# FFN input products by one Strassen step on a normalised input, with the preceding output products in token halves

## The chip, the cores and the metric

The kernel runs on one core of a Trainium2 chip. What counts is the device time of one execution in microseconds (us), as the median of several runs. The engines that matter are TensorE (PE, matrix products into PSUM), VectorE (DVE), ScalarE (ACT), GpSimd (POOL) and the DMA queues, of which SyncE's (SP) carries the weights.

## The reference

The kernel computes one inference step of a two-layer backbone for 640 tokens (512 latent, 128 context) of width 1024. Each layer is FFN 1, a mixer (pooling, convolution, attention) and FFN 2. Cut to the part that the change touches:

```python
m = silu(cond) @ mod_w + mod_b                # 9 modulation vectors of 1024, per layer and kind of token
def ffn(x, shift, scale, gate, wi, wo):       # wi 1024 x 5632, wo 2816 x 1024
    h = rms(x, norm_g) * (1 + scale) + shift  # rms: x / sqrt(mean(x*x)) * norm_g
    g, up = split(h @ wi, 2)                  # two times 2816 columns
    return x + 0.5 * gate * ((silu(g) * up) @ wo)
# per layer: x = ffn 1; x = x + g2 * concat(pool, conv, attn) @ w_out; x = ffn 2
```

All data are float32.

## The kernel before

X holds the residual stream transposed: 8 chunks of 128 features by 640 tokens. Every product in float32 is made as three products of two parts: a matrix is rounded to a high part (`f_wh`, `f_h`, a ScalarE copy) and the rest becomes a low part (`f_wl`, a VectorE subtraction), and high by high, high by low and low by high are summed in PSUM. The 640 tokens are two halves of 320, one PSUM bank each.

An FFN has 44 input chunks of 128 columns (22 of the gate, 22 of the other factor, named `f{layer}{place}_{pair}_{part}{chunk}`; a pair is 256 columns of each part). A weight tile `wi` of 1 MB holds 256 columns; `raw` tiles have three buffers. A chunk is 8 × 3 × 2 = 48 matmuls (line 356). The moving operand `xa` is X times the modulation's scale, not normalised, and two further columns hold the shift; the factor 1/rms (`R`, lines 300 to 313) is multiplied into the product's output in PSUM (lines 392 and 393), the shift's share is added there too, and silu, the gating (line 436) and the split of the hidden chunk (lines 438 and 439) follow. The output products run in four groups of hidden chunks (`GROUPS`, 6, 6, 6 and 4), each over the 8 output chunks m, and each adds into X (line 398, `o_a` and `o_b` are the two halves). A group of output products stands one pair of input chunks behind the hidden chunks that it reads.

The modulation vectors are 72 loads of 1 MB (`mw`). Those at the start are products of 64 columns (line 259). Most of the others are "summed": eight VectorE rows per load accumulate into `ma` (line 225), then a few small products. The code calls one such step at each input weight tile and each pair of output chunks while steps are left (`more`), others inside the mixer.

A scheduler with a look-ahead of 200 (`AHEAD`) arranges each engine's instructions; the order in this document is what it made. The rows of the end of the mixer and of the end of an FFN update X chunk by chunk and at once prepare the next `xa` chunk (`xa_chunk`) and the sum of squares (`sq_chunk`, GpSimd line 382).

Of the kernel before, what the change touches and what calls it, by code (L numbers as in the profile page):

```python
# [95 lines left out]
def backbone(ctx: ExitStack, tc: tile.TileContext, ins, consts, y_prompt, y_sample, out_k, out_v):  # L96
# [106 lines left out]
    def modulation(l, v, summed):  # L203
# [3 lines left out]

        def step(t):
            raw = wpool.tile([P, 2, D], F32, tag="raw", name=f"mw_{l}_{v}_{t}", bufs=3)
# [4 lines left out]
            if summed:  # L214
                if t == 0:
                    st["acc"] = [[half(f"ma_{l}_{v}_{i}{q}") for q in range(2)] for i in range(2)]
                for kk in range(2):
                    k = 2 * t + kk
                    for i in range(2):
                        for q in range(2):  # L220
                            acc, src, c = st["acc"][i][q], raw[:, kk, 512 * q:512 * q + 512], C[:, k, i:i + 1]
                            if k == 0:
                                V.tensor_scalar(out=acc, in0=src, scalar1=c, scalar2=None, op0=ALU.mult)
                            else:
                                V.scalar_tensor_tensor(out=acc, in0=src, scalar=c, in1=acc, op0=ALU.mult, op1=ALU.add)
                if t < 3:
                    return
                ps = bank(f"mod_{l}_{v}", "x")
                for q in range(2):
                    for i in range(2):  # L230
                        w = st["acc"][i][q].rearrange("p (j g c) -> p j g c", g=4, c=32)
                        for g in range(4):
                            PE.matmul(ps[32 * g:32 * g + 32, 128 * q:128 * q + 128], pick[i], w[:, :, g, :], start=(i == 0), stop=(i == 1))
            else:
                if t == 0:
                    st["ps"] = bank(f"mod_{l}_{v}", "x")
                ps = st["ps"]
                for kk in range(2):
                    k = 2 * t + kk
                    w = raw[:, kk, :].rearrange("p (j g c) -> p j g c", g=4, c=32)  # L240
                    for g in range(4):
                        PE.matmul(ps[32 * g:32 * g + 32, 0:256], C[:, k, :], w[:, :, g, :], start=(k == 0), stop=(k == KD - 1))
                if t < 3:
                    return
            mt = half(f"modT_{l}_{v}", 256)
            V.transpose(out=mt, in_=ps[:, 0:256])
            b = mod_b[l][:, v * KD:(v + 1) * KD].unsqueeze(2).to_broadcast([P, KD, 2])
            V.tensor_tensor(out=modv[l][:, v], in0=mt.rearrange("p (j c) -> p j c", c=32)[:, :, 0:2], in1=b, op=ALU.add)
# [743 lines left out]
```

## Time and profile before

| what | value |
|---|---|
| timed runs, median of 3 | 2519.34 us (2518.88 to 2521.01) |
| profiled execution | 2518.95 us |
| its span, first to last instruction | 2517.2 us |
| mean granted TensorE clock | 0.984 of full speed |
| TensorE busy | 2438.6 us, 97% |
| VectorE busy | 1441.7 us, 57% |
| ScalarE busy | 823.5 us, 33% |
| GpSimd busy | 214.1 us, 9% |

The span is shorter than the time, since it counts from the first to the last instruction alone. Busy shares are means over stages with different limits.

### The profile page before, as it was taken

What the parts mean: (1) busy time and instruction counts of PE and PEld (TensorE: products, weight loads), DVE (VectorE), ACT (ScalarE), POOL (GpSimd) and SP (SyncE); (2) the same over time, 40 slices, a digit from 0 to 9 for tenths busy, and PEclk for the clock granted to TensorE, in tenths of its full rate; (3) what the DMA queues carried; (4) which work ended last, traced back from release to release, by engine and by line L of the source; (5) the groups of instructions that cost most, each with busy time, mean ns of one, the idle gap of its engine ahead of it and who ended that gap; (6) DMA issues with size and microseconds to landing.
All of it is one profiled execution on the core that took longest, in us unless ns stands there. A gap on an engine that the chain in (4) does not pass through costs nothing. (4 is left out here: it accounts for less than half of the span.)

```text
span 2517.2 us, 40160 instructions
## 1 busy us (share of the span) xinstructions
PE 2438.6 (97%) x17151; PEld 2343.7 (93%) x17151; DVE 1441.7 (57%) x2878; ACT 823.5 (33%) x1334; POOL 214.1 (9%) x168
## 2 busy tenths in 40 slices
PE   7999999999879999999999999999997899999999
PEld 6999999998569999999999999999885799999999
DVE  6774434468858877734374443446598664444444
ACT  3222222236664222212242122224357542121212
POOL 2000000012531000000010000001124210000000
PEclk8999999999889999999999999999999899999999
DMA  9443222233503344422132222222333131212222
GB/s 291 143 147 107 64 82 67 68 103 107 178 26 114 138 133 152 151 84 68 59 95 74 76 76 76 76 68 76 117 107 130 43 101 59 93 59 84 68 67 68
DMA packets 195919, 245.10 MB, mean 97 GB/s; under 512 B 5721, under 2 KB 178558, under 8 KB 195740
## 3 DMA queue, kind: packets, MB, share of 16 engines
q1 hardware_dynamic: 193904, 240.81, 29.1%
q8 instruction: 134, 2.20, 0.4%
q0 software_dynamic: 368, 1.07, 0.1%
q10 hardware_dynamic: 1468, 0.66, 0.1%
q14 instruction: 45, 0.37, 0.0%
HBM read 239.63 MB, written 2.88 MB: 96 GB/s over the span
## 5 line engine op out<-in xcount | busy, mean ns | idle before, releaser
L356 PE MATMUL f_a<-xa_h,f_wl 128*128 128x320 f32 x1384 | 430.5, 311 | 2.9 <-DVE f_wl L336 2.9
L356 PE MATMUL f_a<-xa_h,f_wh 128*128 128x320 f32 x1384 | 431.2, 312 | 1.1 <-DVE f_t L392 0.7
L356 PE MATMUL f_b<-xa_h,f_wh 128*128 128x322 f32 x1384 | 432.0, 312 | 0.0
L356 PE MATMUL f_b<-xa_h,f_wl 128*128 128x322 f32 x1384 | 431.5, 312 | 0.0
L356 PE MATMUL f_b<-xa_l,f_wh 128*128 128x322 f32 x1384 | 430.6, 311 | 0.2 <-DVE xa_l L374 0.2
L356 PE MATMUL f_a<-xa_l,f_wh 128*128 128x320 f32 x1384 | 429.2, 310 | 0.0
L356 PE MATMUL o_a<-f_h,o_wh 128*128 128x320 f32 x1408 | 423.4, 308 | 0.0
L356 PE MATMUL o_b<-f_h,o_wh 128*128 128x320 f32 x1408 | 422.9, 308 | 0.0
L335 ACT ACTIVATE f_wh<-wi 128x1024 fp32r<-128x1024 f32 x175 | 185.4, 1060 | 705.0 <-PE f_b L356 460.9
L392 DVE TENSOR_TENSOR f_t<-f_a,r 128x320 f32<-128x320 f32 x176 | 86.0, 491 | 540.2 <-PE f_a L356 537.9
L356 PEld LDWEIGHTS f_a<-xa_h,f_wl 128*128 128x128 f32 x1384 | 262.1, 189 | 4.9 <-DVE f_wl L336 3.9
L356 PEld LDWEIGHTS f_a<-xa_h,f_wh 128*128 128x128 f32 x1384 | 262.8, 190 | 2.9 <-ACT f_wh L335 1.1
L356 PEld LDWEIGHTS o_a<-f_h,o_wh 128*128 128x128 f32 x1408 | 263.6, 187 | 1.2 <-ACT o_wh L335 1.0
L356 PEld LDWEIGHTS o_b<-f_h,o_wh 128*128 128x128 f32 x1408 | 263.6, 187 | 0.0
L356 PEld LDWEIGHTS f_a<-xa_l,f_wh 128*128 128x128 f32 x1384 | 262.1, 189 | 0.0
L356 PEld LDWEIGHTS f_b<-xa_h,f_wh 128*128 128x128 f32 x1384 | 261.8, 189 | 0.4 <-issue 0.3
L356 PEld LDWEIGHTS f_b<-xa_l,f_wh 128*128 128x128 f32 x1384 | 261.1, 189 | 0.5 <-DVE xa_l L374 0.5
L356 PEld LDWEIGHTS f_b<-xa_h,f_wl 128*128 128x128 f32 x1384 | 261.0, 189 | 0.2
L335 ACT ACTIVATE o_wh<-wo 128x768 fp32r<-128x768 f32 (+1 forms) x128 | 101.2, 792 | 438.7 <-PE o_b L356 309.0
L336 DVE TENSOR_TENSOR f_wl<-wi,f_wh 128x1024 fp32r<-128x1024 f32 x175 | 215.2, 1230 | 12.2 <-ACT f_wh L335 8.2
L398 DVE SCALAR_TENSOR_TENSOR X<-o_a,gate,X 128x320 f32<-128x320 f32 x128 | 70.2, 549 | 259.9 <-PE o_a L356 259.7
L356 PE MATMUL o_a<-f_h,o_wl 128*128 128x320 f32 x704 | 217.0, 308 | 1.9 <-DVE o_wl L336 1.7
(420 smaller groups left out, 3976.2 us busy)
## 6 DMA issues: line engine op xcount, KB each, us to landing
wi<-in_ffn_wi_dram SPq DMA_DIRECT2D x86, 1024.0 KB, 5.2
mw<-in_mod_w_dram SPq DMA_DIRECT2D x72, 1024.0 KB, 5.8
wo<-in_ffn_wo_dram SPq DMA_DIRECT2D x48, 768.0 KB, 4.7
wo<-in_ffn_wo_dram SPq DMA_DIRECT2D x16, 512.0 KB, 3.6
wout<-in_w_out_dram SPq DMA_DIRECT2D x32, 256.0 KB, 3.0
win_q<-in_w_in_dram SPq DMA_DIRECT2D x4, 1024.0 KB, 5.0
xt<-in_x_sample_dram SPq DMA_DIRECT2D x4, 512.0 KB, 5.8
wi<-in_ffn_wi_dram SPq DMA_DIRECT2D x4, 512.0 KB, 10.1
```

The source lines that it names most:

```text
L335: A.activation(out=wh, in_=src, func=AF.Copy)
L336: V.tensor_tensor(out=wl, in0=src, in1=wh.bitcast(F32), op=ALU.subtract)
L356: PE.matmul(ps[:, :n], ww[:, k, :], xx[:, lo:lo + n], start=(k == order[0] and i == 0), stop=(k == order[-1] and i == 2))
L392: V.tensor_tensor(out=t[:, :HALF], in0=pa[:, :HALF], in1=R[:, :HALF], op=ALU.mult)
L398: V.scalar_tensor_tensor(out=X[:, m, s:e], in0=ps[:, s - o:e - o], scalar=gate[:, m, c:c + 1], in1=X[:, m, s:e], op0=ALU.mult, op1=ALU.add)
```

## The change

The input products of an FFN are made by one step of Strassen's scheme in Winograd's form. The contraction is taken in pairs of 128-feature blocks (even and odd, four pairs kp), a group of 256 columns in two halves, and the tokens in two halves; of eight products of blocks, seven are left, called P1, P2, q6, n5, q7, m4 and q3 (`FORMS`). For this:

- The input is normalised, scaled and shifted before the products (`rstd_half`, `half_input`), since the scheme adds blocks of both token halves. From it seven combinations per k-pair are made and split (`forms_first` for the first half, `forms_second` when the second is there).
- For each group g of 22 per FFN the weights are seven half tiles of 512 columns per partition (`weights`: a ScalarE copy and a VectorE subtraction); four are sums of blocks, t1 and t2 on VectorE, t3 and t4 on GpSimd (`sums`, `run`).
- The products' results are combined on VectorE (in `run`, `second`, `last`): V, U, then the four blocks. The product m4 of a group stands in the next group (`late`).
- The output products that feed an FFN's input (the mixer's last part, and FFN 2's last group in layer 0) run first for tokens 0 to 319, then for 320 to 639 (`last_group`); the first half is normalised meanwhile, and P1 and P2 of the first two groups (`early`) stand before the second half's normalisation (`into_ffn`).
- The modulation steps stand at places that are listed (`fill`): after groups 1 to 5 of the first FFN, and after the odd m of the first two or three output groups of three FFNs; a summed step now takes 512 columns of four k-blocks. At the start all eight modulation tiles come before any product.
- `raw` has two buffers instead of three, split weights three instead of two, `act` six instead of eight. Tiles of an FFN and of a mixer share one region (`phase`), and a table of constants is loaded per mixer.

```diff
-BUFS = {"act": 8, "tmp": 7, "half": 9}
+BUFS = {"act": 6, "tmp": 7, "half": 9, "w": 3, "raw": 2}
...
+        def weights(self, g, form, src):
...
+            h, lo = self.slots.pop(0)
+            A.activation(out=h, in_=src, func=AF.Copy)
+            V.tensor_tensor(out=lo, in0=src, in1=h.bitcast(F32), op=ALU.subtract)
...
+            V.tensor_tensor(out=t1, in0=self.block(g, 0, 0), in1=self.block(g, 0, 1), op=ALU.add)
+            V.tensor_tensor(out=t2, in0=t1, in1=self.block(g, 1, 1), op=ALU.add)
+            G.tensor_tensor(out=t3, in0=self.block(g, 1, 1), in1=self.block(g, 0, 1), op=ALU.add)
...
+            for kp in range(4):
+                for n, (w, f) in enumerate(((h, 0), (h, 1), (lo, 0))):
+                    PE.matmul(ps[:, :HALF], w[:, kp, :], self.F[f][kp][:, i, :], start=(first and kp == 0 and n == 0), stop=(kp == 3 and n == 2), skip_group_check=not first)
...
+            t1, t2, t3 = self.sums(g)
+            self.weights(g, "q6", t2)
+            self.multiply(g, "q6", d, True)
+            V.tensor_tensor(out=v, in0=d[:, :HALF], in1=v, op=ALU.subtract)
+            G.tensor_tensor(out=t2, in0=t2, in1=self.block(g, 1, 0), op=ALU.add)
+            st["t4"] = t2
+            self.weights(g, "n5", t1)
+            self.multiply(g, "n5", B, True)
+            u = half(nm + "_U", HALF)
+            V.tensor_tensor(out=u, in0=B[:, :HALF], in1=v, op=ALU.add)
+            if self.late is not None:
+                self.last(self.late)
+            self.weights(g, "q7", t3)
+            self.multiply(g, "q7", Cb, True)
+            V.tensor_tensor(out=o[1][:, HALF:], in0=Cb[:, :HALF], in1=u, op=ALU.add)
+            if not done:
+                self.second(g)
+            self.weights(g, "q3", self.block(g, 1, 1))
+            self.multiply(g, "q3", B, False)
+            V.tensor_tensor(out=o[1][:, :HALF], in0=B[:, :HALF], in1=v, op=ALU.add)
+            self.hidden(g, 1, slice(0, T))
...
+        def then(h):
+            if h == 1:
+                for g in range(2):
+                    f.early(g)
+            pb = rstd_half(acc, h, f"r{l}{j}{h}")
+            for kp in range(4):
+                if h == 0:
+                    hp.append(forms_first(F, af, pb, kp, f"hf{l}{j}"))
+                else:
+                    forms_second(F, af, pb, kp, hp[kp], f"hf{l}{j}")
...
+        V.tensor_tensor(out=g[:, 0], in0=hq[:, 0], in1=hq[:, 1], op=ALU.add)
+        V.tensor_tensor(out=g[:, 1], in0=hp[:, 0], in1=g[:, 0], op=ALU.subtract)
+        V.tensor_tensor(out=g[:, 2], in0=hq[:, 0], in1=hp[:, 0], op=ALU.subtract)
+        V.tensor_tensor(out=g[:, 3], in0=hp[:, 1], in1=g[:, 1], op=ALU.subtract)
...
-        fill = [late_parameters] + mod_steps(0, [v for v in (2, 4, 3, 5, 7, 6, 8) if v not in FILL_MODS[0]]) if l == 0 else []
...
+            fill = {"steps": [late_parameters] + mod_steps(0, (2, 4, 3))}
+            fill.update({("g", g, False): 1 for g in range(1, 6)})
+            fill.update({("o", gi, m): 1 for gi in range(2) for m in range(1, 8, 2)})
...
+            fill = {"steps": mod_steps(1, (4, 3))}
+            fill.update({("o", gi, m): 1 for gi in range(2) for m in range(1, 8, 2)})
...
+        fill = {"steps": [] if last else mod_steps(l + 1, (1, 0, 2))}
...
+            fill.update({("o", gi, m): 1 for gi in range(3) for m in range(1, 8, 2)})
```

**A group in the middle of the first FFN, VectorE.** Before, a chunk of pair 4 and the next pair's first weights (the names end with the tile's number):

```order
L392 TENSOR_TENSOR f00_4_11_t_2432<-f00_4_11_a_2382,r00_688 128x320
L391 COPY f00_4_11_b_2433<-f00_4_11_b_2383 128x2
L393 TENSOR_TENSOR f00_4_11_t_2432<-f00_4_11_b_2383,r00_688 128x320
L336 TENSOR_TENSOR f00_5_01_wl_2507<-wi00_5_0_2442,f00_5_01_wh_2506 128x1024
L436 SCALAR_TENSOR_TENSOR f00_4_11_t_2432<-f00_4_11_t_2432,f00_4_11_b_2433,f00_4_01_s_2309 128x512
L436 SCALAR_TENSOR_TENSOR f00_4_11_t_2432<-f00_4_11_t_2432,f00_4_11_b_2433,f00_4_01_s_2309 128x128
L439 TENSOR_TENSOR f00_4_11_h_2439<-f00_4_11_t_2432,f00_4_11_h_2439 128x640
```

After, from the sums of group 16 on, with what group 15 still has to do (a split tile holds two forms and bears the name of the first; A, B, C and D are PSUM banks):

```order
L530 TENSOR_TENSOR f00_16_t1_3779<-f00_16_3620 128x512
L531 TENSOR_TENSOR f00_16_t2_3780<-f00_16_t1_3779,f00_16_3620 128x512
L520 TENSOR_TENSOR f00_16_q6_wl_3786<-f00_16_t1_3779,f00_16_q6_wh_3785 128x512
L615 TENSOR_TENSOR f00_15_1_3642<-f00_15_B_3644,f00_15_V_3639 128x320
L520 TENSOR_TENSOR f00_16_q6_wl_3786<-f00_16_t2_3780,f00_16_q6_wh_3785 128x512
L573 TENSOR_TENSOR f00_15_1_3642<-f00_15_1_3642,f00_14_1_3507 128x640
L520 TENSOR_TENSOR f00_15_m4_wl_3820<-f00_15_t2_3647,f00_15_m4_wh_3819 128x512
L520 TENSOR_TENSOR f00_16_P2_wl_3856<-f00_16_3620,f00_16_P2_wh_3855 128x512 x2
L520 TENSOR_TENSOR f00_15_m4_wl_3820<-f00_16_t3_3781,f00_15_m4_wh_3819 128x512
L576 TENSOR_TENSOR f00_15_h1_3752<-f00_15_1_3642,f00_15_h1_3752 128x640
L599 TENSOR_TENSOR f00_16_V_3772<-f00_16_D_3776,f00_16_V_3772 128x320
L520 TENSOR_TENSOR f00_17_P1_wl_3891<-f00_17_3755,f00_17_P1_wh_3890 128x512
```

The subtraction of 1024 columns per chunk has become seven of 512 per group with two sums ahead of them, and the factor r00 on the output is gone.

**The end of the first output group of FFN 2 in layer 0, VectorE.** Before, the last chunk of the group, with modulation steps and the next pair's weights between:

```order
L225 SCALAR_TENSOR_TENSOR ma_1_4_11_9527<-mw_1_4_1_9662,C_79,ma_1_4_11_9527 128x512
L398 SCALAR_TENSOR_TENSOR X_67<-o02_0_7_a_9479,gate_0_2_7934,X_67 128x320
L398 SCALAR_TENSOR_TENSOR X_67<-o02_0_7_b_9480,gate_0_2_7934,X_67 128x192
L398 SCALAR_TENSOR_TENSOR X_67<-o02_0_7_b_9480,gate_0_2_7934,X_67 128x128
L225 SCALAR_TENSOR_TENSOR ma_1_4_00_9524<-mw_1_4_1_9662,C_79,ma_1_4_00_9524 128x512
L336 TENSOR_TENSOR f02_4_01_wl_9599<-wi02_4_0_9520,f02_4_01_wh_9598 128x1024
```

After, the last chunk, the last step of the group and the next group's sums and first split (six rows of `ma` between the first two and the transpose are alike and not shown):

```order
L417 SCALAR_TENSOR_TENSOR X_67<-o02_0_7_b_9588,gate_0_2_8348,X_67 128x128
L240 SCALAR_TENSOR_TENSOR ma_1_1_01_9526<-mw_1_1_3_9628,C_79,ma_1_1_01_9526 128x512
L240 SCALAR_TENSOR_TENSOR ma_1_1_11_9527<-mw_1_1_3_9628,C_79,ma_1_1_11_9527 128x512
...
L220 STREAM_TRANSPOSE modT_1_1_1_9647<-mod_1_1_1_9638 128x128
L530 TENSOR_TENSOR f02_7_t1_9674<-f02_7_9581 128x512
L222 TENSOR_TENSOR modv1_170<-modT_1_1_1_9647,mod_b1_920 128x8
L531 TENSOR_TENSOR f02_7_t2_9675<-f02_7_t1_9674,f02_7_9581 128x512
L299 SCALAR_TENSOR_TENSOR af_1_0_0_12540<-modv1_170,vec_97 128x16
L520 TENSOR_TENSOR f02_7_q6_wl_9681<-f02_7_t1_9674,f02_7_q6_wh_9680 128x512
```

The eight rows of a step now stand in one piece between the group's last residual and the sums that the next group's second product needs.

**The way from the mixer of layer 0 into FFN 2, VectorE.** Before, the last output chunk of the mixer (`p0_1_7`), the first weights and the last chunk of the moving operand:

```order
L336 TENSOR_TENSOR f02_0_00_wl_7953<-wi02_0_0_7936,f02_0_00_wh_7952 128x1024
L398 SCALAR_TENSOR_TENSOR X_67<-p0_1_7_a_7864,gate_0_1_7601,X_67 128x320
L398 SCALAR_TENSOR_TENSOR X_67<-p0_1_7_b_7865,gate_0_1_7601,X_67 128x192
L398 SCALAR_TENSOR_TENSOR X_67<-p0_1_7_b_7865,gate_0_1_7601,X_67 128x128
L336 TENSOR_TENSOR f02_0_01_wl_8015<-wi02_0_0_7936,f02_0_01_wh_8014 128x1024
L374 SCALAR_TENSOR_TENSOR xa02_l_7564<-X_67,a_0_2_7561,xa02_h_7563 128x512
```

After, from the end of the second half's 1/rms (`r021`) to the first combinations of the second half (`hf02_q`, `hf02_g`) and their split into the moving operand (`F02_l`):

```order
L311 SCALAR_TENSOR_TENSOR r021_y2_8281<-r021_w2_8278,r021_y1_8276 128x3
...
L520 TENSOR_TENSOR f02_0_q7_wl_8395<-f02_0_8184,f02_0_q7_wh_8394 128x512
L558 TENSOR_TENSOR f02_1_0_8242<-f02_1_A_8227,f02_0_0_8205 128x320
L445 TENSOR_TENSOR r021_dg_8283<-con_68,r021_y2_8281 128x256
L447 TENSOR_SCALAR r021_dg_8283<-con_68,r021_y2_8281 128x64
L467 TENSOR_TENSOR hf02_q0_8288<-X_67,r021_b_8286 128x640
L490 TENSOR_TENSOR hf02_g0_8294<-hf02_q0_8288,hf02_p0_8018 128x320
...
L478 TENSOR_TENSOR F02_l0_7807<-hf02_g0_8294,F02_h0_7803 128x1280
```

Before, the first product of the FFN needs X chunk by chunk and no 1/rms; after, all products but P1 and P2 need the second half's normalisation, four combinations per k-pair and their split.

## Rows read from the trace of the kernel before

**Rows 1.** The page: span, busy shares, and two rows of the forty slices.

```profile
span 2517.2 us, 40160 instructions
PE 2438.6 (97%) x17151; PEld 2343.7 (93%) x17151; DVE 1441.7 (57%) x2878; ACT 823.5 (33%) x1334; POOL 214.1 (9%) x168
PE   7999999999879999999999999999997899999999
PEclk8999999999889999999999999999999899999999
```

**Rows 2.** Timeline of VectorE, 385 to 430: start, duration, instruction, [idle before <- releaser].

```profile
389.87 1.23 DVE L336 TENSOR_TENSOR f_wl<-wi,f_wh 128x1024 fp32r<-128x1024 f32 x1
391.01 1.01 DVE L436 SCALAR_TENSOR_TENSOR f_t<-f_t,f_b,f_s 128x512 f32<-128x512 f32 x2
...
403.13 0.49 DVE L392 TENSOR_TENSOR f_t<-f_a,r 128x320 f32<-128x320 f32 x1 [4.92 <-PE f_a L356]
...
410.27 0.49 DVE L392 TENSOR_TENSOR f_t<-f_a,r 128x320 f32<-128x320 f32 x1 [4.90 <-PE f_a L356]
...
411.14 0.95 DVE L336 TENSOR_TENSOR o_wl<-wo,o_wh 128x768 fp32r<-128x768 f32 x1
412.00 1.01 DVE L436 SCALAR_TENSOR_TENSOR f_t<-f_t,f_b,f_s 128x512 f32<-128x512 f32 x2
...
422.67 0.55 DVE L398 SCALAR_TENSOR_TENSOR X<-o_a,gate,X 128x320 f32<-128x320 f32 x1 [0.89 <-PE o_a L356]
...
423.73 0.95 DVE L336 TENSOR_TENSOR o_wl<-wo,o_wh 128x768 fp32r<-128x768 f32 x1
427.95 0.55 DVE L398 SCALAR_TENSOR_TENSOR X<-o_a,gate,X 128x320 f32<-128x320 f32 x1 [3.28 <-PE o_a L356]
```

**Rows 3.** Two kinds of split: durations in ns, min/median/max, first and last start.

```profile
L336 DVE TENSOR_TENSOR p_wl<-wout,p_wh x32: 673/684/1681, 680.3 to 2031.0; 128x512 fp32r<-128x512 f32 x32
...
L336 DVE TENSOR_TENSOR f_wl<-wi,f_wh x175: 1208/1225/1868, 22.1 to 2466.2; 128x1024 fp32r<-128x1024 f32 x175
```

**Rows 4.** A GpSimd sum's durations, and the timeline of VectorE and GpSimd at 641.

```profile
L501 POOL TENSOR_TENSOR qr_sh<-qr_sh,con x8: 1272/1282/1773, 571.9 to 1878.5; 128x512 f32<-128x512 f32 x8
...
641.00 0.16 DVE L289 TENSOR_TENSOR rq_w<-rq_y 128x10 f32<-128x10 f32 x1
...
642.94 1.60 POOL L616 TENSOR_TENSOR cy<-cy,cm 128x655 f32<-128x655 f32 x1 [2.70 <-ACT cm L615]
...
643.10 1.46 DVE L289 TENSOR_TENSOR rq_w<-rq_y 128x10 f32<-128x10 f32 x1
```

**Rows 5.** Start: PE timeline; stretches: length, PE, PEld (others), clock, DMA, GB/s; then L344.

```profile
51.24 1.10 PE L259 MATMUL mod<-mw,C 128*32 128x64 f32 x64
...
54.19 0.39 PE L356 MATMUL f_a<-xa_h,f_h 128*128 128x320 f32 x1
...
0.00:54.19 54.19, 37.72 (x656) 33.03 (x656) 34.44 (x78) 18.75 (x35) 16.67 (x18) 0.87 0.94 289
...
0.00:54.19 54.19, 16.28 (x84) 13.81 (x84) 0.87 0.94 289
54.19:62.00 7.81, 2.14 (x13) 1.86 (x12) 1.00 0.80 286
```

**Rows 6.** Stretches at the ends of the two mixers; columns as above, PE first.

```profile
800.00:840.00 40.00, 38.38 (x254) 37.08 (x253) 37.97 (x72) 13.41 (x19) 3.24 (x2) 1.00 0.46 158
...
2020.00:2060.00 40.00, 40.00 (x272) 39.68 (x271) 25.85 (x56) 20.05 (x32) 9.88 (x7) 1.00 0.39 127
```

**Rows 7.** Timeline of VectorE in the chain of a 1/rms.

```profile
526.77 0.16 DVE L302 TENSOR_SCALAR r_v<-r_ss 128x5 f32<-128x5 f32 x1
...
528.77 0.17 DVE L292 SCALAR_TENSOR_TENSOR r_y<-r_w,r_y 128x5 f32<-128x5 f32 x1
...
529.05 0.83 DVE L306 TENSOR_TENSOR r_dg<-con,r_y 128x640 f32<-128x640 f32 x1
```

**Rows 8.** The page's modulation loads (KB, us to landing), and the rows of a step.

```profile
mw<-in_mod_w_dram SPq DMA_DIRECT2D x72, 1024.0 KB, 5.8
...
L225 DVE SCALAR_TENSOR_TENSOR ma<-mw,C,ma x224: 736/746/2056, 54.2 to 1060.9; 128x512 f32<-128x512 f32 x112
```

More of the change, by code (lines that the diff above doesn't have):

```diff
@@ L213, in step @@
             )
[L214 to L248, printed above, removed]
+            if t == 0:
+                st["ps"] = bank(f"mod_{l}_{v}", "x")
+            ps = st["ps"]
+            for kk in range(2):
+                k = 2 * t + kk
+                w = raw[:, kk, :].rearrange("p (j g c) -> p j g c", g=4, c=32)
+                for g in range(4):
+                    PE.matmul(ps[32 * g:32 * g + 32, 0:256], C[:, k, :], w[:, :, g, :], start=(k == 0), stop=(k == KD - 1))
@@ new lines, in ffn, with load, main @@
+    def ffn(f, wo, gate, after, fill, last_out=True):
+        l, j = f.l, f.j
+        jobs, gi = [], 0
+        for g in range(NH):
+            out = []
+            if (g % 2 == 0 and gi < len(GROUPS) - 1 and g >= GROUPS[gi][1]) or g == NH - 1:
+                out = [("o", gi, m) for m in range(KD)] if last_out or gi < len(GROUPS) - 1 else []
+                gi += 1
+            jobs.append(("g", g, bool(out) or g == NH - 1))
+            jobs += out
+        raws = {}
+        def load(job):
+            if job[0] == "g":
+                f.load(job[1])
+            elif job[2] % 2 == 0:
+                lo, hi = GROUPS[job[1]]
+                mp = job[2] // 2
+                raws[job[1], mp] = raw_tile(wo[lo * P:hi * P, mp * 256:(mp + 1) * 256], hi - lo, f"wo{l}{j}_{job[1]}_{mp}")
+        def main(job):
+            if job[0] == "g":
+                f.run(job[1], job[2])
+                return
+            _, gi, m = job
+            lo, hi = GROUPS[gi]
+            w = split_w(raws[gi, m // 2], hi - lo, m % 2, f"o{l}{j}_{gi}_{m}")
+            pa, pb = product(w, lambda k: (f.hid[lo + k][:, 0, :], f.hid[lo + k][:, 1, :]), hi - lo, 0, f"o{l}{j}_{gi}_{m}")
+            residual(pa, pb, m, gate())
+            if gi == len(GROUPS) - 1:
+                after(m)
+        load(jobs[0])
+        for i, job in enumerate(jobs):
+            if i + 1 < len(jobs):
+                load(jobs[i + 1])
+            main(job)
+            for _ in range(fill.get(job, 0)):
+                fill["steps"].pop(0)()
+        assert not fill["steps"], len(fill["steps"])
@@ L597, in mixer @@
         QS, rq = {}, {}
-        ys = [work.tile([P, COUT], F32, tag="sg", name=f"cy{l}{c}", padded_shape=[P, TMP], bufs=3) for c in range(2)]
+        ys = [scope["pool"].tile([P, COUT], F32, tag="sg", name=f"cy{l}{c}", padded_shape=[P, TMP], bufs=3) for c in range(2)]
         todo = [list(range(TAPS)), list(range(TAPS))]
```

408 lines of the change are left out of this document (274 added, 134 removed).

## Prediction, made blind

> **What bounds the kernel now.** I read the page first: TensorE is busy 97% of a span of 2517.2 us, VectorE 57%, and the forty slices show that TensorE's holes are few: the start, and the two mixers [rows 1]. The profiled execution took 2518.95 us, 1.75 more than its span; the median of the timed runs is 2519.34, so I make the sum against 2518.95 and add 0.4 to it. VectorE's rows in a steady stretch then give the unit prices. Two first-half results of neighbouring FFN input chunks stand at 403.13 and 410.27: 7.14 us a chunk, in which TensorE issues 48 matmuls. Two of an output chunk stand at 422.67 and 427.95: 5.28 us for 36 matmuls of 320 columns, so 0.1467 us each [rows 2]. In the same rows VectorE waits 4.9 us before the result. So in the FFNs TensorE alone sets the pace, and VectorE, ScalarE and the loads hide. Nothing waits for the normalisation either: 1/rms is applied to the product's output (line 392), and across the ends of the mixers TensorE is busy for 38.38 and 40.00 of 40.00 us [rows 6].
>
> **Removed.** An FFN has 22 column groups of 256. Before, a group is two chunks, 14.27 us. After, it is 7 block products of 4 k-pairs, 3 terms and 320 columns: 84 matmuls × 0.1467 = 12.32 us. Four FFNs have 88 groups: 88 × 1.95 = 171 us, if TensorE still never waits.
>
> **Does VectorE keep up in a group?** Its work grows, so this decides the size of the gain. The durations overlap: a row of 768 elements with 0.95 us lets its successor start after 0.86, one of 1024 with 1.23 after 1.14 [rows 2], so I take 0.6 us for 512 elements (0.68 alone [rows 3]), 0.4 for 320 and 0.75 for 640. A pair of groups has 14 splits and 4 sums of 512 (18 × 0.6 = 10.8), 9 combinations of 320 out of PSUM (3.6), two with a sign (0.9), and 2.6 of gating and splitting the hidden chunks: 17.9, or 8.97 a group against 12.32. GpSimd adds two sums of 512, 1.28 each [rows 4]. There the trace warns: a VectorE row of ten elements took 1.46 us while a GpSimd sum ran, and 0.16 without one; some 1024-element splits took 1.87 instead of 1.23 [rows 3, 4]. If every GpSimd sum stops VectorE in full, a group has 8.97 + 2.56 = 11.5 us, still under 12.32. But a product cannot start before its sum is made, copied by ScalarE and subtracted, and walking the new order of one pair of groups by these durations I get some 25.0 us without and 25.8 with the GpSimd stops, not 24.6. I take 12.8 a group: 88 × (14.27 − 12.8) = **+129 us** (bounds 12.4 and 13.6: +165 and +59).
>
> The Trainium skill, SBUF — State Buffer, in the section on its two separate sides, calls the port pair of the two engines an exclusive lock that a VectorE operation with two SBUF inputs and a GpSimd one hold for a whole instruction. The rows agree (1.46 against 0.16), and by it the full stop would be the rule: VectorE and GpSimd together would need 11.5 us a group and not 8.97, which leaves the gain at +129 while 12.8 covers it.
>
> **Added: the start.** Before, the last modulation matmuls stand at 51.24, and by 54.19 TensorE had already done 84 products of the first input chunks, 12.3 us of work, since these need only scaled tokens [rows 5]. After, no product can start before both halves are normalised, shifted, combined and split. All eight modulation tiles come first (the DMA engines were 94% busy up to 54.19 [rows 5], so they come no sooner), and behind the last stand a transpose, the affine columns, the last k-pair's combination and split on VectorE (4.2 us, below) and the first weights: some 9 us, so about 61 us with nothing done instead of 54.2 with 12.3 done: **−19** (−12 to −27; two raw buffers instead of three make the loads wait for their consumers).
>
> **Added: three joins.** FFN 2 of layer 0, FFN 1 and FFN 2 of layer 1 begin with the second token half's output products (96 × 0.1467 = 14.1 us from T0), with the first two groups' P1 and P2 as cover (48 matmuls, 7.0 us, of the first half). Then the chain: the last residual at T0 + 15, four splits of the first half (4 × 0.75) to 18; square, sum and column sums beside them; eleven tiny rows at a pitch of 0.2 (526.77 to 528.77 [rows 7]) to some 21; six weight rows of 0.6 that stand ahead in VectorE's order, and the combination that waits for the second early group, to some 28; the diagonal (0.83 for 640 elements [rows 7], less for 320), its broadcast, then per k-pair 0.75 + 4 × 0.4 + 0.4 + 1.42 = 4.2 us of VectorE (1.42 by the pitch of 1.1 ns an element), four times 16.8. That ends at T0 + 47 to 50. TensorE has 14.1 + 7.0 + some 4 us of work till then: 23 idle. The chain before hid but for 1.6 us [rows 6]. Three of them: **−69** (3 × 15 to 3 × 27).
>
> **Moved: the modulation steps.** There are 1 MB loads of 5.8 us median, and eight VectorE rows of 0.746 median each [rows 8]. Before, a step stood beside a whole pair of chunks or of output chunks, where VectorE had room. After, four stand behind groups 2 to 5 of the first FFN, where VectorE's slack is 12.32 − 11.5 = 0.8 us and a step is 5.3 (8 × 0.66 by pitch); with its load sharing two buffers with the weights I take 5 a step: **−20** (−8 to −30). Twenty-eight stand in seven output groups. An output pair is 10.56 us of TensorE; VectorE has two splits, twice the three residual rows (422.67 to 423.73, 1.06 [rows 2]) and the step, 1.7 + 2.1 + 5.3 = 9.1, so nothing is lost inside. At the end something is: the last step's tile takes the buffer of the step before it, its eight rows stand ahead of the next group's two sums and first splits, and its column sums stand on TensorE between that group's first and second product. TensorE has 1.8 us of work there (12 matmuls), VectorE 5.3 + 2.4 and the load's remainder. I take 6.5 each: 7 × 6.5 = **−45** (0 to −70; 0 if the tile lands early enough that the step ends within the last chunk).
>
> **Small.** The mixers keep their work but load through two buffers instead of three: **−10** (0 to −20; there the trace has its holes already). TensorE's granted clock is 0.87 before 54.19 and 1.00 behind [rows 5]; six or seven new gaps will put some matmuls at the lower level: **−8**. The tables that are loaded per mixer go over GpSimd's queue with a whole output group of time: 0. The output rows of the last FFN are unchanged.
>
> Sum: +129 − 19 − 69 − 20 − 45 − 10 − 8 = −42, so 2518.95 + 42 + 0.4 = **2561 us**, slower by 1.7%.
>
> **Rivals.** *Gaps half hidden, so faster.* If the joins cost 15 each, the first FFN's steps 8, the output groups' ends 2 each, and a group 12.6 (+147): 147 − 19 − 45 − 8 − 14 − 10 − 5 = +46, 2473; with a group at 12.8, +28, 2491; I take 2485. What decides is the sum of the gaps: below 129 us of gaps it ends faster. For it: the scheduler reaches far enough to put other products into gaps, as the rows at 2020 to 2060 show. Against: at a join no other work is left that does not need the second half's forms. *VectorE is the bound.* GpSimd's stops fall on the subtractions that feed TensorE, 13.6 us a group: +59 instead of +129, 2631. For it: 1.46 against 0.16; against: 11.5 is less than 12.32. By the Trainium skill's rule on the lock this is what full exclusion would do if the stops also stand on the path. *The arithmetic saves nothing net*: gain and gaps cancel within 0.2%, about what a measurement of this kernel can tell from no change.
>
> **Chances.** Forecast 2561, its own range 2525 to 2615: 0.57. Faster rival (2440 to 2514): 0.26. Same: 0.07. VectorE-bound (2615 to 2680): 0.10. The range for 8 in 10 leaves one in ten at either side: 2468 to 2625. Faster 0.26, same 0.07, slower 0.67.
>
> **What would show it.** Start-to-start of a combination (line 599) in a steady stretch: 12.3 to 12.6 means that VectorE keeps up, 13.6 that it does not. The idle time of TensorE between the second half's last output product and the first full run of a group's products: 23 us at three places. The wait of the second product of a group behind an output group with steps. The first product's start: 61 us. The prediction is wrong if the joins show under 12 us, or if the groups behind output groups start at once.

## The result, and the profile after

The changed kernel takes **2652.62 us** (median of 4, 2652.38 to 2657.19) against 2519.64 (4 runs): ratio 1.0531, interval 1.0513 to 1.0550. It is slower, as forecast, but by 133 us and not by 42; the time lies above the range (2468 to 2625). The rival that VectorE sets every group's pace named nearly this time (2631), with another cause; the rows below speak against that cause, so its nearness is luck. The profiled execution has a span of 2650.8 us.

The page after, in the same rows as [rows 1]:

```profile
span 2650.8 us, 39936 instructions
PE 2390.7 (90%) x16103; PEld 2243.6 (85%) x16103; DVE 1964.8 (74%) x3536; ACT 1039.5 (39%) x1909; POOL 503.9 (19%) x366
PE   4888989999789798989888989899988888999999
PEclk6998999999988799989988989999999888999999
```

TensorE's busy time fell by 48 us only, though 172 us of products (88 groups at 1.95) are gone: its share is now 90%, and 20 of the 40 slices stand under 9 tenths, where before there were five.

A steady stretch of a group block without modulation steps, VectorE's timeline (start, duration, instruction), and behind it the stretches (length, busy and count of TensorE, its loads, VectorE, ScalarE and GpSimd, granted clock, DMA share, GB/s):

```profile
2362.38 0.48 DVE L599 TENSOR_TENSOR f_V<-f_D,f_V 128x320 f32<-128x320 f32 x1
...
2374.42 0.48 DVE L599 TENSOR_TENSOR f_V<-f_D,f_V 128x320 f32<-128x320 f32 x1
...
2387.72 0.48 DVE L599 TENSOR_TENSOR f_V<-f_D,f_V 128x320 f32<-128x320 f32 x1
...
2398.60 0.48 DVE L599 TENSOR_TENSOR f_V<-f_D,f_V 128x320 f32<-128x320 f32 x1
```

```profile
2331.00:2347.00 16.00, 14.01 (x93) 13.26 (x92) 13.47 (x17) 5.19 (x10) 5.81 (x4) 1.00 0.22 67
...
2361.00:2374.00 13.00, 13.00 (x90) 13.00 (x90) 11.89 (x16) 4.93 (x9) 4.33 (x3) 1.00 0.26 82
2374.00:2387.00 13.00, 12.98 (x87) 12.38 (x86) 11.52 (x19) 6.25 (x12) 3.13 (x2) 1.00 0.25 81
```

Three groups from 2362.38 to 2398.60 take 12.07 us each on average, and TensorE is busy for 25.98 of 26.00 us (2361 to 2387): in the middle of a block VectorE keeps up, and the pace is TensorE's own. (The order of the products shifts a little from group to group, so 243 and not 252 lie between the first and the last row; 84 of them take 12.5 us, near the 12.32 of the sum and under the 12.8 that was taken.) The loss sits at the ends. Where the block begins, behind an output group (2331 to 2347), 2 of 16 us are idle.

What the end of an output group without steps looks like, VectorE's and then TensorE's timeline (in brackets the idle time before the row and what ended it):

```profile
2325.85 0.55 DVE L417 SCALAR_TENSOR_TENSOR X<-o_a,gate,X 128x320 f32<-128x320 f32 x1 [4.15 <-PE o_a L375]
2326.31 0.67 DVE L417 SCALAR_TENSOR_TENSOR X<-o_b,gate,X 128x192 f32<-128x192 f32 x2
2326.90 0.68 DVE L530 TENSOR_TENSOR f_t<-f 128x512 f32<-128x512 f32 x1
...
2338.97 0.49 DVE L615 TENSOR_TENSOR f<-f_B,f_V 128x320 f32<-128x320 f32 x1 [2.15 <-PE f_B L540]
...
2340.24 0.68 DVE L530 TENSOR_TENSOR f_t<-f 128x512 f32<-128x512 f32 x1
```

```profile
2328.76 0.41 PE L540 MATMUL f_B<-F_h,f_q_wh 128*128 128x320 f32 x1 [1.04 <-ACT f_q_wh L519]
2341.70 0.42 PE L540 MATMUL f_B<-F_h,f_q_wh 128*128 128x320 f32 x1 [1.89 <-ACT f_q_wh L519]
```

The weight tile had landed long before, as ScalarE's first copy of it shows:

```profile
2311.92 0.63 ACT L519 ACTIVATE f_m_wh<-f 128x512 fp32r<-128x512 f32 x1 [1.22 <-DMA f<-in_ffn_wi_dram]
```

But VectorE idles 4.15 us and takes up the next group's sums only behind the last residual; TensorE then waits for the copy and split of these sums, and once more a group later. The second wait has the same form: VectorE idles 2.15 us before a combination that waits for a product, and the sums of the group after stand behind it, at 2340.24. No run moved that second place. From the first residual of one output group to that of the next are 121.2 us here (2288.9 to 2410.1), where 8 output chunks and 6 groups of products make 42.2 + 73.9 = 116.2.

With a modulation step, the same place in FFN 2 of layer 0:

```profile
1154.97 5.37 DVE L240 SCALAR_TENSOR_TENSOR ma<-mw,C,ma 128x512 f32<-128x512 f32 x8
1161.12 0.32 DVE L220 STREAM_TRANSPOSE modT<-mod 128x128 f32<-128x128 f32 x1 [0.78 <-PE mod L247]
1161.37 0.65 DVE L530 TENSOR_TENSOR f_t<-f 128x512 f32<-128x512 f32 x1
```

```profile
1152.73 0.62 PE L540 MATMUL f_A<-F_h,f_m_wh 128*128 128x320 f32 x1 [2.27 <-ACT f_m_wh L519]
...
1159.83 1.23 PE L247 MATMUL mod<-ma,C 128*32 128x128 f32 x16 [2.73 <-DVE ma L240]
1162.79 0.63 PE L540 MATMUL f_B<-F_h,f_q_wh 128*128 128x320 f32 x1 [1.73 <-ACT f_q_wh L519]
1177.21 0.41 PE L540 MATMUL f_B<-F_h,f_q_wh 128*128 128x320 f32 x1 [1.89 <-ACT f_q_wh L519]
```

Eight rows in one piece (5.37 us, as priced), the column sums on TensorE behind them, and then the sums of the next group: five waits (one is not shown) in place of two. The first of the five is a load, for ScalarE's copy waits for the weight tile to land:

```profile
1152.05 0.63 ACT L519 ACTIVATE f_m_wh<-f 128x512 fp32r<-128x512 f32 x1 [11.55 <-DMA f<-in_ffn_wi_dram]
```

This load was issued only at 1145.48, 5 us before the last output product ends (1150.47); in the empty group it was issued 19 us before (2306.76 and 2325.95). TensorE's products between and behind the waits then run at a lower granted clock, 0.53 here and 1.00 in the same stretch of the empty group (2325.8 to 2339.8):

```profile
1152.00:1166.00 14.00, 8.36 (x39) 6.60 (x40) 12.51 (x22) 4.36 (x8) 3.06 (x3) 0.53 0.31 105
```

Within the group TensorE loses little: its output products take 42.9 us (1107.60 to 1150.47), 42.1 in the empty one (2283.84 to 2325.95). First to last residual are 39.6 us (1114.3 to 1153.9) instead of 36.9 (2288.9 to 2325.8) because the last residual stands behind the late split in VectorE's order.

The join from the mixer of layer 0 into its FFN 2, VectorE's timeline; the last residual of the second half stands at 852.77:

```profile
849.84 3.02 DVE L467 TENSOR_TENSOR hf_p<-X,r_b 128x640 f32<-128x640 f32 x4 [1.32 <-PE r_b L449]
852.77 0.67 DVE L689 SCALAR_TENSOR_TENSOR X<-p,gate,X 128x192 f32<-128x192 f32 x2
...
856.45 0.83 DVE L478 TENSOR_TENSOR F_l<-hf_p,F_h 128x640 fp32r<-128x640 f32 x1 [1.98 <-ACT F_h L477]
857.44 3.06 DVE L478 TENSOR_TENSOR F_l<-hf_p,F_h 128x640 fp32r<-128x640 f32 x2 [0.16 <-ACT F_h L477]
860.42 0.21 DVE L442 TENSOR_SCALAR r_v<-r_ss 128x2 f32<-128x2 f32 x2
...
862.43 0.16 DVE L311 SCALAR_TENSOR_TENSOR r_y<-r_w,r_y 128x3 f32<-128x3 f32 x1
...
869.42 0.49 DVE L558 TENSOR_TENSOR f<-f_A,f 128x320 f32<-128x320 f32 x1
869.83 0.42 DVE L445 TENSOR_TENSOR r_dg<-con,r_y 128x256 f32<-128x256 f32 x1
871.37 0.82 DVE L467 TENSOR_TENSOR hf_q<-X,r_b 128x640 f32<-128x640 f32 x1 [0.96 <-PE r_b L449]
...
889.78 1.49 DVE L478 TENSOR_TENSOR F_l<-hf_g,F_h 128x1280 fp32r<-128x1280 f32 x1 [1.33 <-ACT F_h L477]
892.27 0.49 DVE L599 TENSOR_TENSOR f_V<-f_D,f_V 128x320 f32<-128x320 f32 x1 [0.99 <-PE f_D L540]
```

TensorE's first and last output product of the second half (there are 96), and a stretch of the join:

```profile
834.61 0.45 PE L686 MATMUL p<-mixa,p_wh 128*128 128x320 f32 x2
...
849.79 0.31 PE L686 MATMUL p<-mch,p_l 128*128 128x320 f32 x1
```

```profile
860.00:885.00 25.00, 13.64 (x51) 11.28 (x52) 20.29 (x45) 15.90 (x30) 2.54 (x2) 0.64 0.13 43
```

From the last residual to the first V are 39.5 us (39.3 at the two other joins). TensorE is occupied for 13.64 of 25 us with 51 matmuls, at a mean granted clock of 0.64, which comes to the lower of its two levels (1.2 and 2.4 GHz) for some 70% of the stretch; TensorE had waited 3.57 us before its first cover product at 853.66. [Rows 6] had 38.38 and 40.00 of 40 at this place.

The start, TensorE:

```profile
51.19 1.93 PE L278 MATMUL mod<-mw,C 128*32 128x64 f32 x64 [2.62 <-DMA mw<-in_mod_w_dram]
62.25 0.64 PE L540 MATMUL f_A<-F_h,f_P_wh 128*128 128x320 f32 x1 [9.12 <-ACT F_h L477]
...
66.36 0.63 PE L540 MATMUL f_B<-F_h,f_n_wh 128*128 128x320 f32 x1 [2.05 <-ACT f_n_wh L519]
```

The last modulation matmuls stand where they stood (51.24 in [rows 5]), the first product behind them at 62.25 (61 was forecast), and the products run from 66; the handful before are single k-pairs.

### The profile page after: what moved, and what is told of

It is laid out like the page before. It is cut to its first block, busy times and chain, and to the rows that moved or that the text cites. A ratio compares the mean times of both kernels' runs of the same rounds, so it can differ in the third digit from the quotient of the medians.

```text
span 2650.8 us, 39936 instructions
## 1 busy us (share of the span) xinstructions
PE 2390.7 (90%) x16103; PEld 2243.6 (85%) x16103; DVE 1964.8 (74%) x3536; ACT 1039.5 (39%) x1909; POOL 503.9 (19%) x366
## 3 DMA queue, kind: packets, MB, share of 16 engines
q0 software_dynamic: 512, 1.95, 0.2%
## 4 chain that ended last, share of the span: by engine, by line
PE 61%; DVE 23%; DMA 9%; ACT 5%; issue 2%; POOL 0%; SPq 0%; ACTq 0%; DVEq 0%
PE f_B L540 12%; PE f_A L540 10%; PE f_C L540 10%; DMA mw<-in_mod_w_dram 7%; PE f_D L540 5%; DVE ma L240 5%; PE o_a L375 5%; PE o_b L375 5%; PE p L686 2%; DVE X L417 2%; DVE o_wl L355 2%; PE o L686 1%; PE u_q_a L375 1%; PE u_q_b L375 1%; DVE F_l L478 1%
## 5 line engine op out<-in xcount | busy, mean ns | idle before, releaser
L600 POOL TENSOR_TENSOR f_t<-f_t,f 128x512 f32<-128x512 f32 x88 | 146.0, 1659 | 971.1 <-DVE f_q_wl L520 604.3
L532 POOL TENSOR_TENSOR f_t<-f 128x512 f32<-128x512 f32 x88 | 143.2, 1628 | 610.2 <-DMA f<-in_ffn_wi_dram 542.5
L375 PE MATMUL o_b<-f_h,o_wl 128*128 128x320 f32 x672 | 207.3, 309 | 0.0
L540 PE MATMUL f_B<-F_h,f_q_wh 128*128 128x320 f32 x420 | 146.4, 349 | 50.0 <-ACT f_q_wh L519 49.7
L240 DVE SCALAR_TENSOR_TENSOR ma<-mw,C,ma 128x512 f32<-128x512 f32 x224 | 158.1, 754 | 16.2 <-DMA mw<-in_mod_w_dram 16.0
L520 DVE TENSOR_TENSOR f_q_wl<-f,f_q_wh 128x512 fp32r<-128x512 f32 x128 | 143.9, 1148 | 12.4 <-ACT f_q_wh L519 12.4
L520 DVE TENSOR_TENSOR f_q_wl<-f_t,f_q_wh 128x512 fp32r<-128x512 f32 x164 | 126.5, 784 | 21.1 <-ACT f_q_wh L519 20.1
L540 PE MATMUL f_B<-F_h,f_q_wl 128*128 128x320 f32 x420 | 142.1, 338 | 0.0
L540 PE MATMUL f_B<-F_l,f_q_wh 128*128 128x320 f32 x420 | 141.8, 338 | 0.0
L520 DVE TENSOR_TENSOR f_P_wl<-f,f_P_wh 128x512 fp32r<-128x512 f32 x124 | 129.0, 1068 | 0.3
```

Of the source, the lines that this page charges most:

```text
L375: PE.matmul(ps[:, :n], ww[:, k, :], xx[:, lo:lo + n], start=(k == order[0] and i == 0), stop=(k == order[-1] and i == 2))
L520: V.tensor_tensor(out=lo, in0=src, in1=h.bitcast(F32), op=ALU.subtract)
L532: G.tensor_tensor(out=t3, in0=self.block(g, 1, 1), in1=self.block(g, 0, 1), op=ALU.add)
L540: PE.matmul(ps[:, :HALF], w[:, kp, :], self.F[f][kp][:, i, :], start=(first and kp == 0 and n == 0), stop=(kp == 3 and n == 2), skip_group ...
L600: G.tensor_tensor(out=t2, in0=t2, in1=self.block(g, 1, 0), op=ALU.add)
```

## The experiments

Each experiment's kernel was timed beside the kernel before on the same chip. The price of an edit is the difference of two ratios to the kernel before, times 2519.6 us; the changed kernel's ratio is 1.0531. An interval is about ±0.0018, 4.5 us; a price, the difference of two, is good to some 6.5 us.

**1. The steps of the fills on TensorE.**

```diff
-            fill = {"steps": [late_parameters] + mod_steps(0, (2, 4, 3))}
+            fill = {"steps": [late_parameters] + mod_steps(0, (2, 4, 3), False)}
...
-            fill = {"steps": mod_steps(1, (4, 3))}
+            fill = {"steps": mod_steps(1, (4, 3), False)}
...
-        fill = {"steps": [] if last else mod_steps(l + 1, (1, 0, 2))}
+        fill = {"steps": [] if last else mod_steps(l + 1, (1, 0, 2), False)}
```

> The 32 modulation steps of the fills are made on TensorE (8 small matmuls a step, some 0.7 us of its time) instead of eight VectorE rows each; loads, places and buffers stay. Theory A (VectorE's rows stand ahead of the sums and splits that TensorE waits for): the filled output groups lose some 72 us more than the empty ones, and the groups 2 to 5 of the first FFN some 27, so 2653 - 99 + 22 = 2576 us (2560 to 2595). Theory B (the loads through two buffers make the wait): the loads are the same, so 2640 to 2655.

Measured: 2586.83 us, ratio 1.0285 (1.0267 to 1.0302), 62 us less. Each step is still one load of 1 MB at the same place and in the same buffers (it is cut otherwise, two blocks of 1024 columns instead of four of 512), so VectorE's rows and what they hold up are the price, not the loads as such. The rows hold the two raw buffers too: without them the weight tile's load at the end of this group is issued at 1105.82, 11 us before the last output product ends (1116.52), and the first of the five waits is gone. TensorE's timeline at the end of the same output group as above now has the two waits of the empty one, to the hundredth:

```profile
1120.51 0.41 PE L540 MATMUL f_B<-F_h,f_q_wh 128*128 128x320 f32 x1 [1.04 <-ACT f_q_wh L519]
1133.45 0.42 PE L540 MATMUL f_B<-F_h,f_q_wh 128*128 128x320 f32 x1 [1.89 <-ACT f_q_wh L519]
```

**2. No steps at all.**

```diff
-            fill = {"steps": [late_parameters] + mod_steps(0, (2, 4, 3))}
-            fill.update({("g", g, False): 1 for g in range(1, 6)})
+            fill = {"steps": [late_parameters]}
+            fill.update({("g", 1, False): 1})
...
+    V.memset(modv[0][:, 2:5], 0.01)
+    V.memset(modv[1][:, 0:5], 0.01)
...
```

> The 32 modulation steps of the fills are left out, loads and all; constants stand for their results. Both theories: the whole price of the fills, 2653 - 100 = 2553 us (2535 to 2570); under A this is some 20 us under the run with the steps on TensorE, under B some 100. What is left above the kernel before is then joins, start and the ends of output groups: +35 us.

Measured: 2551.63 us, ratio 1.0145 (1.0130 to 1.0160): all the fills together cost 97 us, 62 of which are VectorE's share of experiment 1. The 35 that remain are about what the steps then take on TensorE itself: its output products pause 0.93 us for each (1081.26 to 1082.19 in experiment 1), 30 us for 32 steps. The first residual of the program, here and in the changed kernel:

```profile
160.27 0.55 DVE L419 SCALAR_TENSOR_TENSOR X<-o_a,gate,X 128x320 f32<-128x320 f32 x1 [4.06 <-PE o_a L377]
```

```profile
189.65 0.55 DVE L417 SCALAR_TENSOR_TENSOR X<-o_a,gate,X 128x320 f32<-128x320 f32 x1
```

So the steps behind groups 2 to 5 cost 29; the stretches of the filled output groups are 8 to 14 us shorter, 73 in sum over seven.

**3. The join's dependency.** The second half's forms are made from the first half, so its 1/rms and residuals are not waited for.

```diff
+                return
             pb = rstd_half(acc, h, f"r{l}{j}{h}")
             for kp in range(4):
-                if h == 0:
-                    hp.append(forms_first(F, af, pb, kp, f"hf{l}{j}"))
-                else:
-                    forms_second(F, af, pb, kp, hp[kp], f"hf{l}{j}")
+                hp.append(forms_first(F, af, pb, kp, f"hf{l}{j}"))
+            for kp in range(4):
+                forms_second(F, af, pb, kp, hp[kp], f"hf{l}{j}", 0)
...
```

(the `return` stands in the branch of the second half; the last argument makes the second half's input from the first half's tokens)

> At the three joins the second token half's operand is made from the first half's tokens and normalisation, so it waits neither for the second half's output products nor for its 1/rms; the amount of work is the same but for the small 1/rms chain. Theory A (the chain behind the last residual): a join loses some 31 us more than before the change, and of that 17 us of VectorE's combinations can now lie beside the 21 us of products: 2653 - 3 x 22 = 2587 us (2570 to 2600). Rival (it is the amount of VectorE's work at the join, and the clock): 2635 or more.

Measured: 2636.31 us, ratio 1.0476 (1.0455 to 1.0496), 14 us less: the rival's 2635. Theory A, as written, fell, but at the joins themselves the edit did more than the time shows. From the last residual to the first V are 29.7, 29.8 and 30.0 us instead of 39.5, 39.3 and 39.3, some 29 less in sum (theory A had 22 each); the two FFNs with steps behind a join took 8 and 5 us longer in this run (969.3 to 1364.8 against 980.9 to 1368.2, and 1482.9 to 1866.1 against 1496.2 to 1874.3), which stays unexplained. What is left at a join is still 30 us. VectorE's timeline shows why:

```profile
847.79 3.02 DVE L467 TENSOR_TENSOR hf_p<-X,r_b 128x640 f32<-128x640 f32 x4 [1.32 <-PE r_b L449]
...
851.46 0.67 DVE L689 SCALAR_TENSOR_TENSOR X<-p,gate,X 128x192 f32<-128x192 f32 x2
...
878.13 2.39 DVE L478 TENSOR_TENSOR F_l<-hf_g,F_h 128x1280 fp32r<-128x1280 f32 x1 [1.34 <-ACT F_h L477]
881.18 0.49 DVE L599 TENSOR_TENSOR f_V<-f_D,f_V 128x320 f32<-128x320 f32 x1 [0.66 <-PE f_D L540]
```

Even the first half's 1/rms is there only at 847.79, 4 us ahead of the second half's last residual, and from then on VectorE and ScalarE have 33 us of forms, weights and copies. The second half's output products cover the first half's own 1/rms, and of the forms hardly more than the first rows.

**4. Less VectorE work at the join.** The low parts of the four combinations g are left out; products that need one take another low part.

```diff
-        split_form(F, kp, 3, g, 4)
+        A.activation(out=F[0][kp][:, 3:7, :], in_=g, func=AF.Copy)
...
```

> The low parts of the four combinations g are left out (their VectorE split of 1280 elements, 1.42 us by pitch, four times at each of the three joins and at the start; the products take another low part in their place, so their number stays). Theory E (between the first half's 1/rms and the first full group VectorE has some 30 us of rows without a break, so each us of it counts): 4 places x 5 us, 2653 - 20 = 2633 us (2625 to 2638). Rival A (the second half's chain in its order is what counts, the splits lie beside ScalarE's copies): 2646 or more.

Measured: 2635.59 us, ratio 1.0465 (1.0449 to 1.0480), 17 us less. The last residual and the first V of the first join:

```profile
855.68 0.67 DVE L689 SCALAR_TENSOR_TENSOR X<-p,gate,X 128x192 f32<-128x192 f32 x2
...
890.00 0.49 DVE L599 TENSOR_TENSOR f_V<-f_D,f_V 128x320 f32<-128x320 f32 x1 [1.64 <-PE f_D L540]
```

The three joins are 34.3, 34.1 and 34.0 us from residual to V instead of 39.5, 39.3 and 39.3, and the first V of the program stands at 70.6 instead of 74.3: 5.2 us at a join for 5.7 us of rows. So at a join VectorE's rows count nearly in full, and rival A falls.

**5. The sums of the group behind an output group written ahead of its last chunk.**

```diff
-            t1, t2, t3 = self.sums(g)
+            t1, t2, t3 = st["sums"] if "sums" in st else self.sums(g)
...
                 load(jobs[i + 1])
+                nj = jobs[i + 1]
+                if job[0] == "o" and nj[0] == "g":
+                    f.g[nj[1]]["sums"] = f.sums(nj[1])
```

> The three sums of the group behind an output group are written ahead of that group's last output chunk instead of behind it. Theory A (in an empty output group TensorE waits 2.9 of 5.0 us for the split of sums that stand behind the last residual; in a filled one behind eight more rows): 11 places, 3 us at the 4 empty ones and 6 at the 7 filled ones: 2653 - 54 = 2599 us (2590 to 2630). Rival (the rows are only exchanged, VectorE has no room there): 2648 to 2656.

Measured: 2618.61 us, ratio 1.0409 (1.0393 to 1.0424), 31 us less. TensorE's wait of 1.04 at the end of an empty group is gone, the one of 1.89 a group later stands; the filled stretches of FFN 2 in layer 0 fell from 133.4 and 133.0 to 129.1 and 129.3, the empty ones of layer 1 by 0.5 and 3.0. The rows were not only exchanged: VectorE had room (the 4.15 idle us above), in the wrong place.

**6. GpSimd's sums on VectorE.**

```diff
-            G.tensor_tensor(out=t3, in0=self.block(g, 1, 1), in1=self.block(g, 0, 1), op=ALU.add)
+            V.tensor_tensor(out=t3, in0=self.block(g, 1, 1), in1=self.block(g, 0, 1), op=ALU.add)
...
-            G.tensor_tensor(out=t2, in0=t2, in1=self.block(g, 1, 0), op=ALU.add)
+            V.tensor_tensor(out=t2, in0=t2, in1=self.block(g, 1, 0), op=ALU.add)
```

> The two weight sums of a group that GpSimd makes (t3 and t4) go to VectorE. By the trace of the changed kernel the 616 splits of 512 elements lost 572 - 616 x 0.68 = 153 us to GpSimd's sums, and 176 sums on VectorE add 106: VectorE works 47 us less. Theory A (in the middle of a block of groups TensorE is full anyway, VectorE is late only beside fills and behind output groups): some 15 of the 47 are seen, 2638 us (2625 to 2648). Rival C (the stops set the pace of every group, as the VectorE-bound rival of the prediction has it): 47 or more, at most 2606. Rival D (t3 is later in VectorE's order, TensorE waits for it): 2655 or more.

Measured: 2646.11 us, ratio 1.0503 (1.0485 to 1.0520). The difference of 7 us is within the two intervals; at most some 16 is possible, and the 47 of the VectorE-bound rival is excluded.

**7. Two raw buffers in the kernel before.**

```diff
-        raw = wpool.tile([P, nk, 256], F32, tag="raw", name=name, padded_shape=[P, KD, 256], bufs=3)
+        raw = wpool.tile([P, nk, 256], F32, tag="raw", name=name, padded_shape=[P, KD, 256], bufs=2)
```

(and so at the five other places of that tag)

> The kernel before with two buffers of raw weights instead of three, nothing else. Theory A (VectorE's rows, not the loads, made most of the loss): 2516 + 5 to 20, the mixers and the start above all, where the changed kernel lost 12 in the second mixer. Theory B (two buffers are a main cause): 2516 + 40 or more.

Measured: 2533.52 us, ratio 1.0054 (1.0039 to 1.0069): 14 us. From the last output residual of FFN 1 to the last residual of the mixer, layer 1 takes 287.0 us instead of 277.9; the changed kernel takes 290.4. Layer 0 shows nothing of the kind (285.2, 284.0 and 283.4). So two buffers alone are a small part of the loss, as theory A said; what they cost in the changed kernel, where VectorE's rows hold them longer, no run shows.

**8. Edits 1, 5 and 6 together.**

> Three edits together: modulation steps on TensorE, sums ahead of the last output chunk, all sums on VectorE. Theory A: the first two have shown 66 and 34, which partly lie at the same places (the ends of the filled output groups), so some 80 of the 100 stay, and 10 more from the sums: 2653 - 90 = 2563 us (2550 to 2575), still slower than before by the joins and the start. Rival: they add up in full, 2540 or less.

Measured: 2562.55 us, ratio 1.0169 (1.0154 to 1.0184), 91 us less, of the 100 that the three give one by one (62, 31 and 7).

**9. The diagonal ahead.** At a join it stood behind a combination for 7.3 us (862.43 to 869.83 above).

```diff
-        dg = tmp(name + "_dg", HALF)
+        dg = half(name + "_dg", HALF)
...
-            pb = rstd_half(acc, h, f"r{l}{j}{h}")
+            with tc.high_priority(offset=AHEAD):
+                pb = rstd_half(acc, h, f"r{l}{j}{h}")
```

> The diagonal of 1/rms takes a buffer of another tag and the 1/rms chain a higher priority, so that at a join the diagonal stands ahead of the six weight rows and of the combination that waits for the second early group (7.3 us in the trace of the changed kernel). Theory A (the chain of the second half is what TensorE waits for): the diagonal comes 7 us sooner, but four of the rows behind it must still run before the forms can be split, so 1 to 4 us a join: 2653 - 8 = 2645 us (2640 to 2650). Rival E (the amount of VectorE's work from the first half's forms on sets the join, in whatever order): 2651 to 2654.

> The combination of three edits (2562.6) with the diagonal moved ahead as well. Theory A: 2562 - 8 = 2554 us (2549 to 2560); rival E: 2561 to 2564. Slower than the kernel before in either case: two buffers in the mixers 14, the start 20, the joins some 70 to 85 remain.

Measured: 2657.88 us, ratio 1.0551 (1.0531 to 1.0570), no gain; with the three edits 2556.62, ratio 1.0150 (1.0129 to 1.0172), not distinct from 1.0169. The traces show two things at once: the joins fell to 37.6, 37.7 and 36.3 us (6.5 in sum, the 1 to 4 each that was expected), and the first V of the program moved from 74.3 to 83.6. That the new buffer did this at the start, and not the priority, is shown by the next run.

**10. The same, with the start left alone** (the edit against the kernel of experiment 9, the other three as in 8).

```diff
-        dg = half(name + "_dg", HALF)
+        dg = tmp(name + "_dg", HALF) if name[1:3] == "00" else half(name + "_dg", HALF)
```

> As the four edits together, but at the start the diagonal keeps its old buffer, since in the two runs with the new one the first V of the program came 9.3 us later (83.6 instead of 74.3) while the three joins were 6.5 us shorter in sum. Theory: 2557 - 9 = 2548 us (2544 to 2554). Rival (the late start is the priority's doing, or changes from build to build): 2554 to 2562.

Measured: 2551.21 us, ratio 1.0128 (1.0112 to 1.0145), the first V again at 74.5, with the priority kept. It is the best version found, 101 us under the changed kernel and still 32 above the one before.

## Why the prediction was wrong

The sum, term by term. The measured terms come from the elapsed time between residuals of output groups (VectorE's first `o_a` rows) in both traces, less the products in between (0.1467 us each after, 7.14 an input chunk before). For the start, as an example: the first output residual stands at 160.3 us without steps (experiment 2), 7 groups and an output chunk are 91.5, so 68.8 are lost; before, 167.7 less 16 input chunks and an output chunk (119.5) is 48.2; the difference is 21. The 69 us at the ends of output groups are what is left over when the other terms are taken out, net of what the kernel before lost at the same places.

| step of the prediction | forecast, us | measured, us |
|---|---|---|
| groups at 12.8 instead of 14.27 | +129 | +103 (172 of products, −69 at the ends of output groups) |
| start | −19 | −21 |
| three joins, 23 each | −69 | −101 |
| steps behind groups 2 to 5 | −20 | −29 |
| steps in seven output groups | −45 | −73 |
| mixers with two buffers | −10 | −12 |
| clock | −8 | in the rows above |
| sum | −42 | −133 |

All signs were right, and the start, the mixers and the products removed came out. Three steps failed, and no single one made the error: the group's pace (26 us too good), the three joins (32) and the price of the modulation steps (37). The clock's 8 us lie inside the measured rows.

**The group's pace.** The step "I take 12.8 a group" spread a loss evenly that is not there in the middle (12.07 between 2362 and 2399, TensorE full) and sits at the twelve ends of output groups, 69 us in all (5.0 at the empty one shown above). The walk had taken a pair from the middle and never a group behind output products. Experiment 5 shows that a part is the order of the sums; the wait of 1.89 us a group later has the same order behind it in the rows, but no run moved it.

**The joins.** The rows and their order were as forecast, and one stretch of the chain was too short. T0 is 834.6, where the second half's output products begin; they end at 850.1. The step that failed is "the last residual at T0 + 15, four splits of the first half (4 × 0.75) to 18": the last residual stands at T0 + 18.2, since the four rows that make the first half's input (`hf_p`, 3.02 us) run ahead of it, and the splits end at T0 + 25.9, since they wait for ScalarE's copies (1.98 us before one of them). From there the chain took the time that was forecast, 8 us late: the diagonal at T0 + 35.2 instead of 28, the end of the last split at T0 + 56.7 instead of 47 to 50, the first V at T0 + 57.7. The prediction also left out that TensorE does the work it has there at a granted clock of 0.64, so that the cover is worth less. Experiment 3 shows how much of a join is the wait for the second half at all: 10 of 39 us, 14 us of the kernel's time for all three; experiment 4 shows that VectorE's rows count almost one for one. So the larger part is the amount of work between the first half's 1/rms and the first full group. The 101 are taken up to the first output residual behind a join, so what the groups between lose is in them.

**The fills.** 65 was forecast and 102 came (97 by experiment 2's ratio). The price of the steps at the end of an output group ("I take 6.5 each") was thought of as one wait; it came to 73 for seven, 10.4 each. The trace has five waits in place of two, among them the weight tile's late landing (2.27) and the column sums (2.73) ahead of the next group's sums, and products at a granted clock of 0.53 between them. "Nothing is lost inside" the output group held: 42.9 us of TensorE against 42.1. Experiment 1 shows that VectorE's rows, with the raw buffers that they hold up, are the main part; whether a third buffer alone would have brought the tile in time was not run.

**The rivals.** VectorE-bound at 13.6 a group: 2631 lies near the time, but the middle of a block is full on TensorE, and experiment 6 returns 7 us, within the noise, not the 47 or more that this rival asks for. What the Trainium skill (SBUF — State Buffer, the section on two separate sides) calls an exclusive lock agrees with the trace (1.74 and 1.78 us for two rows that overlap, where 1.28 and 0.69 are the times alone). Its price was still nearly nothing: VectorE's rows that a GpSimd sum stops are mostly late within a slack.

```profile
2368.56 1.74 POOL L600 TENSOR_TENSOR f_t<-f_t,f 128x512 f32<-128x512 f32 x1 [6.66 <-DVE f_q_wl L520]
```

```profile
2369.07 1.78 DVE L520 TENSOR_TENSOR f_m_wl<-f_t,f_m_wh 128x512 fp32r<-128x512 f32 x1
```

The faster rival needed gaps under 129 us; they came to 236, and the ends of output groups took 69 of the gain besides.

**What stays open.** How the 101 of the joins divide between the lower clock and the waiting itself, why experiment 3 lost elsewhere what it won at the joins, and what a third raw buffer would give in the changed kernel.

## What to carry to other kernels

A scheme that saves products takes its operand's preparation with it: here each point where the normalised input is made costs some 30 us of VectorE and ScalarE, while the 22 groups of an FFN give back 1.95 us each at best, 43 in all, so count the joins before the groups. Price an edit at the seams of the program (behind a block, at the first group, beside the filling work) and not in the steady middle, where everything fits. And work that hid beside a slack engine must be moved when the slack goes: the modulation steps beside the FFNs cost some 8 us before (one stretch between output groups of 136.1 us, 1064.2 less 928.1, where the others are 127 to 128), 97 us here, and 35 once TensorE made them.

## What the runs showed of the hardware

A GpSimd sum and VectorE stop each other: splits of 512 elements took 0.69 us where no sum ran and up to 1.78 beside one, and most of the sums themselves 1.62 to 1.74 against the 1.28 of [rows 4]; over the program VectorE's 616 splits lost 153 us to it (572 less 616 × 0.68), and moving the 176 sums to VectorE returned 7. At the joins the clock was granted at 0.64 in the stretch in which TensorE waited, at 0.53 at the end of an output group with steps, and at 1.00 in the steady stretch of layer 1; before, the mean was 0.984, after, 0.934.
